# Projection steps, rotation engine and first loads in a four-layer trunk: one change in four places

## The chip, the cores and the metric

The kernel runs on one core of one Trainium2 chip. The metric is the device time of one execution in microseconds. A run's time is a little longer than the span of its trace, which reaches from the first to the last instruction.

## The reference

The reference is a trunk of four residual layers over 512 tokens with 1024 features, all in float32, each with an RMS norm ahead of it.

- An even mixer: stick-breaking attention with 16 heads of width 64, strictly causal. Its weights are `sigmoid(z)` times the product of `sigmoid(-z)` over the later keys in front of the query.
- A SwiGLU feed-forward layer with 2816 hidden features: `(silu(h Wg) * (h Wu)) Wd`.
- An odd mixer: differential attention with 8 heads. Every head has two query-key maps of width 64 and one v of width 128. q and k get an RMS norm per group of 64, then a partial rotation of their first 16 features by the positions; the two softmax maps are combined as `a1 - lam * a2`; the head's output is normed again.
- A second SwiGLU layer.

## The kernel before, in words

**Precision.** Every float32 product is made of three TensorE products of rounded halves (`mm3`, line 215): high times high, high times low, low times high. So each operand exists as a pair `hi`, `lo`. Weights are split on arrival in one of two ways. `wload` (line 105) fetches the raw weights over SP's queue into a tile of tag "raw" (two buffers), rounds them on ScalarE to `hi`, and subtracts on VectorE to get `lo`. `wload_acc` (line 115) writes `hi` and `-hi` on ScalarE and then lets GpSimd's queue fetch the weights a second time with an accumulating transfer, which leaves `lo`. Five pairs of 1024 columns are there at a time (`WB`).

**The order of the work.** The kernel is written as one program for a scheduler which makes the semaphores and the order on each engine. The place in the program is the priority: an engine takes the earliest instruction that is ready by the scheduler's own timeline, so later work can run ahead of its place where engines would be idle. Each engine then runs that order as it is. Tiles of one tag share a fixed number of buffers. Later work is also mixed in by hand: `fillers` holds generators of matmul steps, `fill(n)` (line 227) takes n steps from them, `flush` (line 235) takes all up to one generator.

**The start** (lines 86 to 95 and 390 to 478). x comes as 8 tiles of 128 x 512 over SP's queue, mixed with the first pair's q and k weights in quarters (lines 402 to 408). ScalarE and VectorE make the 16 halves of the scaled x (`Norm.scaled`), which stay in tiles of tag "t" of the pool with `HP` = 26 buffers. TensorE runs the first q and k. Then come the first v chunk (`v_chunk(0)`, lines 428 to 449, weights by `wload_acc` on line 446) and the norm's root and broadcast (`Norm.finish`, line 183).

**A head of attention** is a call of `attend` (line 371): scores and weights of the four query blocks from the last to the first (`weigh(3)` to `weigh(0)`), between them the end of the head before (`after`), the transposes of the weights (`wt_bank`), four calls `fill(steps[i])`, and `middle`. The weights times v (`av`) follow.

**The odd layer** (`diff_layer`, line 707) works on four pairs of heads. `qk_steps(c)` (line 750) makes q and k of pair c: 4 token blocks of 512 columns with two yields each, so 8 steps; each block is evicted (line 756), squared into a tile of tag "tmp" (line 758, three buffers in the whole kernel) and reduced (line 759). After the last step come the root, the scaling of the whole tile (line 769) and the rotation: for q and for k four VectorE instructions, two on 128 columns and two on 256 (lines 786 to 789). `v_steps(c)` (line 729) has 4 steps. `head_stacks` (line 792) transposes one head's q and k and splits them into stacks; the k stack is completed by two copies on GpSimd's queue (line 334). `weights` (line 802) takes the softmax maps; its results lie in tiles `e1` with 4 buffers. `head_out` (line 847) finishes a head: transposes, squares into a tile of tag "tmp" (line 861), norm, transposes and halves.

The loop over heads (lines 907 to 926) sets the places. `counts[hd]` says how many steps stand at each of the four calls of `fill`: in the even head 2, 1, 2, 1 and in the odd head 2, 1, 1, 1 for the first three pairs; in the last two heads 1 each, which take the first half of the output projection. `after` of a head is `head_out` of the head before. In an odd head `middle` first flushes the next pair's `qk_steps` and then makes the next head's stacks. `before` flushes the pair's own v.

Of the kernel before, what the change touches and what calls it, by code (L numbers as in the profile page):

```python
# [12 lines left out]
F32 = mybir.dt.float32  # L13
# [4 lines left out]
ALU = mybir.AluOpType  # L18
# [3 lines left out]
P = 128  # L22
S = 512
# [8 lines left out]
ROT = 16  # L32
RSQRT_MAGIC = float(0x5F3759DF)
TCK = dict(schedule_with_timeline_sim=True)
HP = 26
WB = 5
THIRDS = ((0, 8), (8, 8), (16, 6))
TWO_PI_A = 6.28125
# [5 lines left out]
def trunk(  # L44
# [26 lines left out]
    nc = tc.nc  # L71
    V, A, G, T = nc.vector, nc.scalar, nc.gpsimd, nc.tensor
# [10 lines left out]
    x = [xp.tile([P, S], F32, name=f"x{i}") for i in range(KT)]  # L83
# [31 lines left out]
    def wload_acc(ap):  # L115
        raw = raw_tile()
        hi, lo = pair()
        nc.sync.dma_start(out=raw, in_=ap)
        A.activation(hi, raw, AF.Copy)
        A.activation(lo, hi.bitcast(F32), AF.Copy, scale=-1.0)  # L120
        G.dma_start(out=lo, in_=ap, accum_op=ALU.add)
        return hi, lo
# [267 lines left out]
    def stick_layer(norm, nxt):  # L390
        h = norm.h
        with ExitStack() as st:
            vp = st.enter_context(tc.tile_pool(name="vp0", bufs=2))
            sp = st.enter_context(tc.tile_pool(name="sp0", bufs=2))
            at = st.enter_context(tc.tile_pool(name="at0", bufs=2))
# [6 lines left out]
            for j in range(4):  # L402
                c = slice(j * 256, (j + 1) * 256)
                for i, (raw, (hi, lo)) in enumerate(zip(raws, first)):
                    nc.sync.dma_start(out=raw[:, c], in_=wqk0[8 * i][:, c])
                for i in (2 * j + 1, 2 * j + 2):
                    if i < KT:
                        nc.sync.dma_start(out=x[i], in_=xT[i])
            nc.sync.dma_start(out=gf, in_=g_ffn)
            for j in range(4):  # L410
                c = slice(j * 256, (j + 1) * 256)
# [16 lines left out]
            def v_chunk(c):  # L428
                v = vp.tile([P, TT, 4, P], F32R, tag="v", name="v0")

                def evac(t, ps):
                    rs = norm.rstd[:, t : t + 1]
                    src = ps.rearrange("p (h d) -> p h d", d=64)
                    A.activation(v[:, t, :, 0:64], src, AF.Copy, scale=rs)
                    V.scalar_tensor_tensor(
                        v[:, t, :, 64:128],
                        src,
                        rs,
                        v.bitcast(F32)[:, t, :, 0:64],
                        op0=ALU.mult,  # L440
                        op1=ALU.subtract,
                    )

                def steps():
                    yield from nat_steps(
                        [wload_acc(wv0[c, j]) for j in range(2)], h, evac, 256, 1
                    )

                return v, steps()
# [257 lines left out]
    def diff_layer(norm, nxt):  # L707
        h = norm.h
        with ExitStack() as st:
# [40 lines left out]
            def qk_steps(c, out):  # L750
                t_ = qp.tile([P, TT, S], F32, tag="qk", name="qk_nat")
                ss = sm.tile([P, 32], F32, tag="rs_v", name="qk_ss")

                def evac(t, ps):
                    norm_ready()
                    A.activation(t_[:, t], ps, AF.Copy, scale=norm.rstd[:, t : t + 1])
                    sq = tmp.tile([P, S], F32, tag="tmp", name="qk_sq")
                    A.activation(sq, t_[:, t], AF.Square)
                    V.reduce_sum(
                        ss[:, t * 8 : (t + 1) * 8],  # L760
                        sq.rearrange("p (g d) -> p g d", d=64),
                        axis=AX.X,
                    )

                yield from nat_steps([wload_kept(("wqk", c, j)) for j in range(4)], h, evac, 512, 2)
                V.tensor_scalar(ss, ss, 1.0 / 64, EPS, op0=ALU.mult, op1=ALU.add)
                u = rsqrt(ss, 32)
                f3 = t_.rearrange("p t (g d) -> p (t g) d", d=64)
                V.tensor_tensor(
                    f3, f3, u.unsqueeze(2).to_broadcast([P, 32, 64]), op=ALU.mult  # L770
                )
                for which in range(2):
                    f4 = t_[:, :, which * 256 : which * 256 + 256].rearrange(
                        "p t (g d) -> p t g d", d=64
                    )
                    ta, tb = (
                        r.unsqueeze(2).to_broadcast([P, TT, 4, ROT]) for r in rot[which]
                    )
                    mt = tmp.tile([P, S], F32, tag="tmp", name="rope")
                    m = [  # L780
                        mt[:, i * 256 : i * 256 + 256].rearrange(
                            "p (t g d) -> p t g d", t=TT, d=ROT
                        )
                        for i in range(2)
                    ]
                    V.tensor_tensor(m[1][:, :, :, 0:8], f4[:, :, :, 8:16], tb[:, :, :, 0:8], op=ALU.mult)
                    V.tensor_tensor(m[1][:, :, :, 8:16], f4[:, :, :, 0:8], tb[:, :, :, 8:16], op=ALU.mult)
                    V.tensor_tensor(m[0], f4[:, :, :, 0:ROT], ta, op=ALU.mult)
                    V.tensor_tensor(f4[:, :, :, 0:ROT], m[0], m[1], op=ALU.add)
                out.append(t_)  # L790

            def head_stacks(qk, hh):
# [9 lines left out]
            def weights(q2, k2, ss, qt):  # L802
                n = (qt + 1) * P
                nm = sm.tile([P, 2], F32, tag="nm", name="nm")
                e1 = at.tile([P, S], F32, tag="e1", bufs=4, name="e1")
                e2 = at.tile([P, S], F32, tag="e2", name="e2")
                for e, o in ((0, e1), (1, e2)):
                    ps = scp.tile([P, S], F32, tag="sc", name="sc")
                    scores(ps, q2, k2, e, qt)
                    V.memset(ps[0:64, n - 64 : n], NEG)  # L810
                    V.reduce_max(nm[:, e : e + 1], ps[:, :n], axis=AX.X, negate=True)
                    A.activation(
                        o[:, :n],
                        ps[:, :n],
                        AF.Exp,
                        bias=nm[:, e : e + 1],
                        accum_out=ss[:, e, qt : qt + 1],
                    )
                c = sm.tile([P, 2], F32, tag="c", name="c")
                V.reciprocal(c[:, 0:1], ss[:, 1, qt : qt + 1])  # L820
                V.tensor_scalar(
                    c[:, 1:2], ss[:, 0, qt : qt + 1], nlam, c[:, 0:1], op0=ALU.mult, op1=ALU.mult
                )
                V.scalar_tensor_tensor(
                    e1[:, :n], e2[:, :n], c[:, 1:2], e1[:, :n], op0=ALU.mult, op1=ALU.add
                )
                return e1
# [76 lines left out]
                gens["v", c] = v_steps(c, vs)  # L904
                fillers.extend((gens["qk", c], gens["v", c]))
            last = out_first(1, og)
            counts = ((2, 1, 2, 1), (2, 1, 1, 1)) * 3 + ((1, 1, 1, 1), (1, 1, 1, 1))
            for hd in range(8):
                hh = hd % 2
                c = hd // 2  # L910
# [109 lines left out]
```

## Time and profile before

| what | value |
|---|---|
| median of 3 runs | 1301.82 us (1300.54 to 1305.36) |
| profiled execution, its own time | 1301.36 us |
| its span | 1299.6 us |
| TensorE busy (PE) | 1239.7 us, 95% |
| VectorE busy (DVE) | 740.2 us, 57% |
| ScalarE busy (ACT) | 568.2 us, 44% |
| GpSimd busy (POOL) | 80.8 us, 6% |
| mean granted clock of TensorE | 0.979 |

The profile names engines as PE (matmuls), PEld (weight loads of TensorE), DVE, ACT, POOL and SP. Instructions are given by the line of the kernel, the tile they write and the tiles they read; a line can be that of a helper. A clock of 1.00 is TensorE's full 2.4 GHz, 0.50 is 1.2 GHz. Matmuls are pipelined, so the duration of one is longer than the distance to the next. By the trace the even mixer fills the first 270 us or so, the first feed-forward layer reaches to about 635 us, the odd mixer to about 931 us, and the second feed-forward layer to the end.

### The profile page before, as it was taken

The numbers are of one execution on the slowest core, as the hardware profiler recorded it, in microseconds if no ns is written. First come the engines' busy times: TensorE is split into PE (matmuls) and PEld (weight loads), VectorE is DVE, ScalarE is ACT, GpSimd is POOL, SyncE is SP. The second block draws the span as 40 slices with busy tenths as digits, with TensorE's granted clock in tenths as the row PEclk, the third lists the DMA queues.
The fourth block names the chain that finished last, engine by engine and source line by source line (L and its number), as shares of the span: only waits on it lengthen the run. The fifth ranks groups of instructions, "written<-read, shape, count | busy, mean of one in ns | idle before, by whom it ended". The sixth has DMA issues, their size and how long they took to land.

```text
span 1299.6 us, 16000 instructions
## 1 busy us (share of the span) xinstructions
PE 1239.7 (95%) x5974; PEld 1032.3 (79%) x5974; DVE 740.2 (57%) x1426; ACT 568.2 (44%) x964; POOL 80.8 (6%) x132
## 2 busy tenths in 40 slices
PE   6999999889999999999999997968899999999998
PEld 5888888778888888888888887745688888888886
DVE  5567868597544554455535657677754434443442
ACT  7777887455332432334324445345443223321220
POOL 1211111000000000000000000000000000000000
PEclk8999999999999999999999998979899999999999
DMA  7965768238776777766557352501222323332222
GB/s 222 220 148 134 169 143 191 58 97 275 247 227 244 242 246 231 243 233 227 196 194 227 131 158 90 174 17 33 97 100 97 95 97 98 98 97 97 93 73 77
DMA packets 61133, 199.44 MB, mean 153 GB/s; under 512 B 8320, under 2 KB 9344, under 8 KB 61056
## 3 DMA queue, kind: packets, MB, share of 16 engines
q1 hardware_dynamic: 42768, 140.74, 33.0%
q0 software_dynamic: 18144, 57.68, 16.8%
q8 instruction: 47, 0.77, 0.2%
q14 instruction: 30, 0.25, 0.1%
q10 hardware_dynamic: 144, 0.01, 0.0%
HBM read 154.36 MB, written 35.65 MB: 146 GB/s over the span
## 4 chain that ended last, share of the span: by engine, by line
PE 90%; DVE 3%; ACT 3%; DMA 2%; issue 1%; SPq 0%; POOL 0%; DVEq 0%; ACTq 0%; POOLq 0%
PE ps_d L217 6%; PE ps_d L216 6%; PE ps_d L218 6%; PE ps_g L218 6%; PE ps_g L216 6%; PE ps_g L217 6%; PE ps_u L218 6%; PE ps_u L216 6%; PE ps_u L217 6%; PE ps_nat L216 4%; PE ps_nat L217 4%; PE ps_nat L218 4%; PE ps_o L216 2%; PE ps_o L217 2%; PE ps_o L218 2%; PE tp L358 2%
## 5 line engine op out<-in xcount | busy, mean ns | idle before, releaser
L109 ACT ACTIVATE whi<-wraw 128x1024 fp32r<-128x1024 f32 (+1 forms) x136 | 138.6, 1033 | 355.8 <-PE ps_d L217 82.4
L110 DVE TENSOR_TENSOR wlo<-wraw,whi 128x1024 fp32r<-128x1024 f32 (+1 forms) x136 | 161.9, 1192 | 106.1 <-ACT whi L109 50.5
L217 PE MATMUL ps_d<-alo,whi 128*128 128x512 f32 x352 | 139.1, 396 | 0.0
L218 PE MATMUL ps_d<-ahi,wlo 128*128 128x512 f32 x352 | 139.0, 396 | 0.0
L216 PE MATMUL ps_d<-ahi,whi 128*128 128x512 f32 x352 | 138.9, 396 | 0.0
L216 PE MATMUL ps_u<-hhi,whi 128*128 128x512 f32 x352 | 137.7, 391 | 0.3 <-DVE x L298 0.2
L218 PE MATMUL ps_g<-hhi,wlo 128*128 128x512 f32 x352 | 137.6, 391 | 0.0
L217 PE MATMUL ps_g<-hlo,whi 128*128 128x512 f32 x352 | 137.2, 390 | 0.0
L218 PE MATMUL ps_u<-hhi,wlo 128*128 128x512 f32 x352 | 137.1, 390 | 0.0
L217 PE MATMUL ps_u<-hlo,whi 128*128 128x512 f32 x352 | 137.1, 390 | 0.0
L216 PE MATMUL ps_g<-hhi,whi 128*128 128x512 f32 x352 | 136.7, 390 | 0.0
L217 PE MATMUL ps_nat<-wlo,hhi 128*128 128x256 f32 (+1 forms) x384 | 124.7, 325 | 7.0 <-DMA wlo<-in_wv 7.0
L216 PE MATMUL ps_nat<-whi,hhi 128*128 128x256 f32 (+1 forms) x384 | 124.5, 326 | 1.1 <-DVE k L453 1.0
L218 PE MATMUL ps_nat<-whi,hlo 128*128 128x256 f32 (+1 forms) x384 | 124.7, 325 | 0.0
L606 DVE TENSOR_TENSOR x<-x,ps_d 128x512 f32<-128x512 f32 x48 | 32.8, 687 | 97.2 <-PE ps_d L218 97.1
L217 PEld LDWEIGHTS ps_nat<-wlo,hhi 128*128 128x128 f32 x384 | 74.1, 193 | 12.5 <-DMA wlo<-in_wv 7.2
L216 PEld LDWEIGHTS ps_nat<-whi,hhi 128*128 128x128 f32 x384 | 74.0, 193 | 7.0 <-DVE k L453 1.2
L217 PEld LDWEIGHTS ps_d<-alo,whi 128*128 128x128 f32 x352 | 66.2, 188 | 15.9
L218 PEld LDWEIGHTS ps_d<-ahi,wlo 128*128 128x128 f32 x352 | 66.2, 188 | 15.9
L216 PEld LDWEIGHTS ps_d<-ahi,whi 128*128 128x128 f32 x352 | 66.2, 188 | 15.9
L218 PEld LDWEIGHTS ps_nat<-whi,hlo 128*128 128x128 f32 x384 | 74.1, 193 | 5.1 <-issue 0.2
L216 PEld LDWEIGHTS ps_u<-hhi,whi 128*128 128x128 f32 x352 | 66.1, 188 | 14.9 <-ACT whi L109 0.6
(206 smaller groups left out, 2328.5 us busy)
## 6 DMA issues: line engine op xcount, KB each, us to landing
wraw<-in_wgu SPq DMA_DIRECT2D x88, 512.0 KB, 3.6
wraw<-in_wd SPq DMA_DIRECT2D x32, 512.0 KB, 3.6
k<-k POOLq DMA_DIRECT2D x32, 256.0 KB, 3.3
praw<-in_wqk SPq DMA_DIRECT2D x16, 512.0 KB, 5.7
kept_wqk<-whi POOLq DMA_DIRECT2D x16, 512.0 KB, 5.5
kept_wqk<-wlo POOLq DMA_DIRECT2D x16, 512.0 KB, 6.6
whi<-kept_wqk SPq DMA_DIRECT2D x16, 512.0 KB, 6.3
wlo<-kept_wqk SPq DMA_DIRECT2D x16, 512.0 KB, 5.9
```

The lines of the kernel that those rows point to most:

```text
L109: A.activation(hi[:, :cols], raw[:, :cols], AF.Copy)
L110: V.tensor_tensor(lo[:, :cols], raw[:, :cols], hi.bitcast(F32)[:, :cols], op=ALU.subtract)
L216: T.matmul(ps, lh[0], rh[0], start=first, stop=False)
L217: T.matmul(ps, lh[0], rh[1], start=False, stop=False)
L218: T.matmul(ps, lh[1], rh[0], start=False, stop=last)
L358: T.transpose(tp[:, o : o + P], w[qt][:, kt * P : (kt + 1) * P], ident)
L606: V.tensor_tensor(x[m], x[m], ps, op=ALU.add)
```

## The change

Five edits are made.

- `counts` for the first three pairs of the odd layer become 3, 3, 3, 3 in the even head and 0, 0, 0, 0 in the odd head.
- The eight rotation instructions of a pair move from VectorE to GpSimd.
- x[1] to x[7] are fetched over GpSimd's queue instead of SP's.
- The two weight tiles of the even layer's first v chunk are split by `wload` instead of `wload_acc`; the other three chunks stay.
- `e1` gets a fifth buffer, and `HP` goes from 26 to 25 (one buffer of either kind is 2 KB a partition).

```diff
--- before.py
+++ after.py
@@ -32,7 +32,7 @@
 ROT = 16
 RSQRT_MAGIC = float(0x5F3759DF)
 TCK = dict(schedule_with_timeline_sim=True)
-HP = 26
+HP = 25
 WB = 5
 THIRDS = ((0, 8), (8, 8), (16, 6))
 TWO_PI_A = 6.28125
@@ -405,7 +405,7 @@
                     nc.sync.dma_start(out=raw[:, c], in_=wqk0[8 * i][:, c])
                 for i in (2 * j + 1, 2 * j + 2):
                     if i < KT:
-                        nc.sync.dma_start(out=x[i], in_=xT[i])
+                        G.dma_start(out=x[i], in_=xT[i])
             nc.sync.dma_start(out=gf, in_=g_ffn)
             for j in range(4):
                 c = slice(j * 256, (j + 1) * 256)
@@ -443,7 +443,11 @@
 
                 def steps():
                     yield from nat_steps(
-                        [wload_acc(wv0[c, j]) for j in range(2)], h, evac, 256, 1
+                        [(wload_acc if c else wload)(wv0[c, j]) for j in range(2)],
+                        h,
+                        evac,
+                        256,
+                        1,
                     )
 
                 return v, steps()
@@ -783,10 +787,10 @@
                         )
                         for i in range(2)
                     ]
-                    V.tensor_tensor(m[1][:, :, :, 0:8], f4[:, :, :, 8:16], tb[:, :, :, 0:8], op=ALU.mult)
-                    V.tensor_tensor(m[1][:, :, :, 8:16], f4[:, :, :, 0:8], tb[:, :, :, 8:16], op=ALU.mult)
-                    V.tensor_tensor(m[0], f4[:, :, :, 0:ROT], ta, op=ALU.mult)
-                    V.tensor_tensor(f4[:, :, :, 0:ROT], m[0], m[1], op=ALU.add)
+                    G.tensor_tensor(m[1][:, :, :, 0:8], f4[:, :, :, 8:16], tb[:, :, :, 0:8], op=ALU.mult)
+                    G.tensor_tensor(m[1][:, :, :, 8:16], f4[:, :, :, 0:8], tb[:, :, :, 8:16], op=ALU.mult)
+                    G.tensor_tensor(m[0], f4[:, :, :, 0:ROT], ta, op=ALU.mult)
+                    G.tensor_tensor(f4[:, :, :, 0:ROT], m[0], m[1], op=ALU.add)
                 out.append(t_)
 
             def head_stacks(qk, hh):
@@ -802,7 +806,7 @@
             def weights(q2, k2, ss, qt):
                 n = (qt + 1) * P
                 nm = sm.tile([P, 2], F32, tag="nm", name="nm")
-                e1 = at.tile([P, S], F32, tag="e1", bufs=4, name="e1")
+                e1 = at.tile([P, S], F32, tag="e1", bufs=5, name="e1")
                 e2 = at.tile([P, S], F32, tag="e2", name="e2")
                 for e, o in ((0, e1), (1, e2)):
                     ps = scp.tile([P, S], F32, tag="sc", name="sc")
@@ -904,7 +908,7 @@
                 gens["v", c] = v_steps(c, vs)
                 fillers.extend((gens["qk", c], gens["v", c]))
             last = out_first(1, og)
-            counts = ((2, 1, 2, 1), (2, 1, 1, 1)) * 3 + ((1, 1, 1, 1), (1, 1, 1, 1))
+            counts = ((3, 3, 3, 3), (0, 0, 0, 0)) * 3 + ((1, 1, 1, 1), (1, 1, 1, 1))
             for hd in range(8):
                 hh = hd % 2
                 c = hd // 2
```

## Rows read from the trace of the kernel before

**Rows 1.** Stretches: length, busy us of PE, PEld, DVE, ACT, POOL; granted clock; DMA; GB/s.

```profile
25.00:30.00 5.00, 2.21 (x10) 2.21 (x11) 0.00 (x0) 2.11 (x2) 0.86 (x1) 0.50 1.04 258
...
690.00:742.00 52.00, 52.00 (x324) 46.64 (x323) 33.97 (x109) 24.11 (x64) 1.17 (x2) 1.00 0.55 190
742.00:906.00 164.00, 135.97 (x711) 110.58 (x710) 116.92 (x376) 77.23 (x219) 6.95 (x12) 0.91 0.32 98
```

**Rows 2.** Order of time at the start: start us, us, engine, line, operation [idle before].

```profile
17.59 1.06 ACT L119 ACTIVATE whi<-wraw 128x1024 fp32r<-128x1024 f32 x1 [1.80 <-DMA wraw<-in_wv]
...
20.07 1.07 POOL L121 DMA_DIRECT2D wlo<-in_wv  x1 [18.76 <-ACT wlo L120]
...
20.18 0.40 PE L218 MATMUL ps_k<-hhi,wlo 128*128 128x512 f32 x1
...
27.79 0.58 PE L217 MATMUL ps_nat<-wlo,hhi 128*128 128x256 f32 x1 [6.98 <-DMA wlo<-in_wv]
...
33.08 1.31 PE L211 MATMUL ps_bc<-dg,ones 128*128 128x512 f32 x2
```

**Rows 3.** TensorE in time: first av product of heads 0, 1, 2, 3, 7.

```profile
718.64 0.39 PE L216 MATMUL av<-wt_hi,v1h 128*128 128x512 f32 x1
...
739.90 0.40 PE L216 MATMUL av<-wt_hi,v1h 128*128 128x512 f32 x1
...
785.96 0.39 PE L216 MATMUL av<-wt_hi,v1h 128*128 128x512 f32 x1
...
799.25 0.77 PE L216 MATMUL av<-wt_hi,v1h 128*128 128x512 f32 x1
...
903.26 0.48 PE L216 MATMUL av<-wt_hi,v1h 128*128 128x512 f32 x1
```

**Rows 4.** ScalarE in time: pair 1's eviction and square, pair 3's square.

```profile
694.42 0.69 ACT L756 ACTIVATE qk_nat<-ps_nat,rstd 128x512 f32<-128x512 f32 x1
...
727.67 0.37 ACT L861 ACTIVATE o_sq<-tn,rs 128x128 f32<-128x128 f32 x1
...
728.01 0.64 ACT L758 ACTIVATE qk_sq<-qk_nat 128x512 f32<-128x512 f32 x1
...
849.54 1.16 ACT L758 ACTIVATE qk_sq<-qk_nat 128x512 f32<-128x512 f32 x2
```

**Rows 5.** Waits of ScalarE, 690 to 906 us: total us, times, longest us.

```profile
ACT e L812 <- PE tp L358: 2.3, 3, 1.1
```

**Rows 6.** Order of time in the even layer around the fifth pair's output.

```profile
187.05 0.69 DVE L533 TENSOR_TENSOR olo<-o,ohi 128x512 fp32r<-128x512 f32 x1
...
190.67 0.39 PE L216 MATMUL ps_k<-hhi,whi 128*128 128x512 f32 x1
...
225.51 0.67 DVE L516 TENSOR_TENSOR o<-av,avt 64x512 f32<-64x512 f32 x1
```

**Rows 7.** Two source lines of the rotation: duration ns min/median/max.

```profile
L786 DVE TENSOR_TENSOR rope<-qk_nat,rot x8: 280/284/291, 666.1 to 861.2; 128x128 f32<-128x128 f32 x8
...
L789 DVE TENSOR_TENSOR qk_nat<-rope x8: 415/418/423, 667.9 to 862.3; 128x256 f32<-128x256 f32 x8
```

**Rows 8.** Order of time around pair 0's rotation and first stack.

```profile
663.45 2.29 DVE L769 TENSOR_TENSOR qk_nat<-qk_nat,rs_u 128x2048 f32<-128x2048 f32 x1
...
667.92 0.75 DVE L789 TENSOR_TENSOR qk_nat<-rope 128x256 f32<-128x256 f32 x2
...
672.61 0.60 PE L798 MATMUL tqk<-ident,qk_nat 128*128 128x128 f32 x4
```

**Rows 9.** Costliest groups on the page: the low halves of the weights.

```profile
L110 DVE TENSOR_TENSOR wlo<-wraw,whi 128x1024 fp32r<-128x1024 f32 (+1 forms) x136 | 161.9, 1192 | 106.1 <-ACT whi L109 50.5
```

**Rows 10.** DMA issue to landing: x to 20 us, wlo 14 to 45.

```profile
DMA to landing us min/median/max: 2.8/4.3/4.6
...
DMA to landing us min/median/max: 6.8/8.3/9.5
```

**Rows 11.** Pair 0's projection and v: the stretch for ps_nat alone.

```profile
634.74:669.56 34.82, 34.07 (x193) 29.55 (x193) 1.44 (x3) 4.16 (x7) 1.00 0.45 161
```

## The prediction

> **What bounds the kernel now.** I read the page's busy shares first (TensorE is busy for 95% of the span, so a change has to remove TensorE idle time or time at the lower clock), then the stretches, to find where that idle time lies. Two places are left. One is the start: in 25 to 30 us TensorE runs at a granted clock of 0.50, which is the 1.2 GHz level, and is busy for less than half of the stretch. The other is the odd layer from its second head on: in 742 to 906 us TensorE is busy for 136.0 of 164 us at a mean clock of 0.91, while from 690 to 742 it had no gap at all [rows 1]. Then I read the order of time in both places.
>
> At the start TensorE ends the first projections at 20.58 us and stands 6.98 us at the second term of v's product, because wlo of v's first weights is fetched by an accumulating transfer. GpSimd issues that at 20.07 us, though the raw weights had been there at 17.59 us, when ScalarE began to round them. The products then run at the lower clock up to the broadcast of the norm at 33.08 us [rows 2].
>
> In the odd layer the cadence of the heads tells more than any single wait. The av products of heads 0 and 1 begin 21.3 us apart (718.64 and 739.90). Head 2 comes 46.1 us after head 1, and head 3 13.3 us after head 2; that long-short pattern stands three times. From head 1 to head 7 the mean is (903.26 - 739.90)/6 = 27.2 us [rows 3]. The reason is in ScalarE's order: the last block of pair 1's q and k was evicted at 694.42 us, but its square was taken only at 728.01 us, directly behind the squares of head 0's output (727.67). The same stands twice more, for pairs 2 and 3, the last at 849.54 us [rows 4]. The tiles of tag "tmp" are given out in the order of the program, and in the program the last projection steps of a pair stand in the odd head behind the call that finishes the head before. So norm, rotation and stacks of the next pair cannot begin before that head is finished, and there is nothing left then to put on TensorE.
>
> **The change, part by part.** The sum goes against the profiled execution, 1301.36 us (span 1299.6 and 1.8 around it); it lies 0.46 us under the median of 1301.82.
>
> Projection steps. A pair's projection has 8 steps and its v 4. With counts of 3 in the even head and 0 in the odd one all 12 stand in the even head, so the four squares of a pair come ahead of that head's own finish and behind the odd head's before it. Pair 1's rotation can end some 30 us sooner (728.01 against 694.42), and pairs 2 and 3 each get one head, 21 us or more, of slack where they have none now. The long interval goes. What is late next is TensorE itself: its 136.0 us of work in these six heads are 22.7 us a head [rows 1, 3]. VectorE's 116.9 us, less two rotations, are 18.5 us a head. I take 23 us a head: (27.2 - 23) x 6 = 25 us. From below: 0, if another wait fills the long interval. From above: at full clock TensorE's 136.0 us shrink by about 9%, to 20.6 us a head, near the 21.3 already shown; 6 x 6.6 = 40 us. I lie on TensorE's present busy time and not on the 20.6, because some idle time stays. What follows the last head I leave as it is. In the odd heads no projection steps are left in program order; they are covered by the next pair's steps, which TensorE already runs ahead of their place (no gap in 690 to 742). If that cover is gone, it is the second rival.
>
> The fifth e1 buffer. ScalarE's exponential waits for the transposes of the head before three times, 2.3 us together [rows 5]. That is the most it shows; it is inside the 23 us. It is paid by a 26th residual buffer: the low half of pair 4's output in the even layer must now wait for the first h tile. It is written at 187.05 us and would come some 4 us later, when pair 7's key projection has begun (190.67); the next pair but one writes into the buffer that it reads only at 225.51 us [rows 6]. So it costs nothing; if that slack were gone, some 4 us.
>
> Rotation on GpSimd. Four instructions like L786 (0.284 us) and four like L789 (0.418) are 2.8 us a pair on VectorE [rows 7], and leave it. On GpSimd no row shows such an operation. Bounds for the pair: 2.8 us, as on VectorE, and 8 x 2.29 = 18.3, if each took as long as VectorE's longest operation on this path, L769 with 2048 columns [rows 8]; on columns of 128 and 256 I lie near the lower end, 6 us. Only pair 0 has it on the way: its last rotation ends at 668.67 us, the stacks' transposes begin at 672.61 [rows 8], and 3.9 us of slack hide 6 - 2.8. Behind it on GpSimd stand the two copies of each k stack; those of the odd head are issued ahead of it, those of the next even head need it anyway. I put it at 0; up to 15.4 - 3.9 = 11.5 us. The Trainium skill (GPSIMD Engine Reference, section 3.1, Elementwise, side-by-side cycle accounting) speaks against this part: an addition of two float32 tensors of 2048 columns takes 4497 ns there against 2293 on VectorE, about twice. VectorE's figure agrees with L769's 2.29 us here [rows 8]; GpSimd's no row here shows. By that rule a pair would take about 5.6 us, an estimate, and the sum would stay as it is.
>
> v's first weights. Without the two transfers the low half is ready at 17.59 + 1.06 + 1.19 (L110's mean [rows 9]) = 19.84 us, before TensorE is free at 20.58. The 6.98 us go. So does the lower clock that followed the gap: the products from 27.79 to 33.08 us, 5.3 us, would take half, 2.6 us less. Against it stand 2.4 us of VectorE work ahead of the norm's root, and what is late next: the weights of the next projection, whose own accumulating transfers land 6.8 to 9.5 us after issue [rows 10] and are wanted some 9 us sooner. They gain from the 1 MB that no longer moves beside them. I take 8.5 us; bounds 4 and 9.6. The even layer behind it keeps TensorE busy, so the shift lasts.
>
> x over GpSimd's queue. Seven issues leave SP. On GpSimd the first issue took 1.07 us, and the engine had been idle for 18.76 us before it [rows 2], so all seven can go out ahead of everything else there. x lands 2.8 to 4.6 us after issue now, the slowest accumulating transfer of GpSimd's queue took 9.5 [rows 10]: between 1.8 us sooner and 4.9 us later for the first x. I take 0, near x's own rows, since both queues move the same bytes at the same time. The first weights come sooner on SP, which is worth nothing while ScalarE rounds both x and them in turn.
>
> Sum: 25 + 8.5 = 33.5 us, so 1268.
>
> **The rivals.**
> Only the start pays. Another thing in program order, such as v's two buffers or the two PSUM banks of the projections, fills the long interval between odd and even head. For it: the scheduler makes its own order, and no row shows the new one. Against it: the square's wait, 33.6 us for pair 1, stands three times in the same place [rows 4]. Time: 1301.4 - 8.5 = 1293.
>
> The projection goes ahead of the even head's own scores, and the odd head stands uncovered. If the plan keeps program order, the 12 steps (34.1 us of products for pair 0 [rows 11]) come between the score blocks of the even head: 34.1 + 13.3, its own work at the shortest interval shown, and then 13.3 for the odd head, which has nothing beside it. That is 60.7 us a pair against 2 x 27.2 now, 6.3 us more for each of the three pairs with a projection behind them: 1301.4 + 18.9 - 8.5 = 1312. It decides from the point where TensorE no longer runs a pair ahead. Against it: in 690 to 742 us TensorE has no gap though the program gives these heads fewer steps than that [rows 1], so order is only a preference.
>
> GpSimd's rotation is exposed. At the upper bound of 18.3 us pair 0's stacks start 11.5 us late, and nothing later gives it back: 1280. The Trainium skill (the same page, section 8, Key points) adds that GpSimd shares its SBUF interfaces with VectorE where VectorE reads two SBUF inputs; no run here shows what that costs.
>
> The start does not pay. x lands late from the software queue, or the first projection's weights do, and 8.5 us become 0 while the heads gain: 1276.
>
> **How the numbers follow.** Chances: forecast 0.64 (by itself 1252 to 1284: 9.6 + 40 us at the one end, 4 + 13 us, half of the cadence's gain, at the other); only the start 0.17, of which 0.07 within 0.5%; own scores behind the projection 0.07, slower; rotation exposed 0.07; no start 0.05. A measurement of this kernel can tell about 0.5%, 6.5 us, from no change. Faster 0.64 + 0.10 + 0.07 + 0.05 = 0.86, same 0.07, slower 0.07. The range takes in the upper bounds and the start alone, 1252 to 1294; the slower rival stays outside.
>
> **What would show it.** Right: no wait of TensorE for wlo at v's first product, and a clock of 1.00 in 25 to 35 us; the square of the last block of a pair behind the finish of the odd head before, not of its own even head; av products of heads 1 to 7 about 23 us apart without the long-short pattern; TensorE busy over 90% from the second head to the last. Wrong: long intervals that remain, with another releaser ahead of the stacks' transposes; TensorE idle in odd heads with VectorE busy; transposes of the stacks that wait for GpSimd; a first projection after v that waits for its own transfer.

## The result and the profile after

The changed kernel takes 1266.1 us (median of 4 runs, 1263.76 to 1268.86) against 1301.55 before: a ratio of 0.9723, interval 0.9695 to 0.9751. The forecast was 1268 in a range of 1252 to 1294. Its profiled execution is the slowest of the four, 1268.86 us, with a span of 1267.0, so the same 1.8 us lie around the span as before. The total is right, and that is partly luck: one of the two large terms under it was put too small and the other did not come at all, and the errors cancel.

Busy shares on the page of the changed kernel:

```profile
PE 1225.4 (97%) x5974; PEld 1024.5 (81%) x5974; DVE 732.2 (58%) x1396; ACT 566.8 (45%) x962; POOL 101.4 (8%) x169
```

TensorE has the same work and less of it at the lower clock (1225.4 us busy against 1239.7); GpSimd has 20 us more. The stretches of the changed kernel show where (columns: stretch, length, busy us of PE, PEld, DVE, ACT, POOL with instructions, granted clock, DMA share, GB/s):

```profile
25.00:30.00 5.00, 4.84 (x36) 4.01 (x35) 3.04 (x8) 4.90 (x7) 1.29 (x2) 1.00 0.77 188
30.00:35.00 5.00, 5.00 (x44) 5.00 (x43) 3.03 (x5) 3.68 (x7) 2.60 (x4) 1.00 1.01 256
40.00:45.00 5.00, 1.05 (x5) 0.55 (x3) 0.00 (x0) 2.01 (x3) 0.88 (x1) 0.94 1.20 242
45.00:50.00 5.00, 4.58 (x12) 3.88 (x13) 2.13 (x3) 4.97 (x8) 0.00 (x0) 0.50 1.04 274
742.00:873.00 131.00, 122.20 (x712) 105.00 (x711) 105.54 (x351) 71.77 (x209) 14.90 (x26) 0.97 0.40 123
```

Against [rows 1], the hole at 25 to 30 us is closed and the clock there is 1.00. The same kind of hole, with the 0.50 clock behind it, now stands at 40 to 50 us. In the odd layer, 742 to 873 us reaches from head 1 to just behind the av of head 7, as 742 to 906 did before: 33 us shorter, TensorE busy for 93% at 0.97 instead of 83% at 0.91.

**The odd layer.** TensorE in time, first av product of heads 0, 1, 2, 3 and 7:

```profile
723.25 0.48 PE L216 MATMUL av<-wt_hi,v1h 128*128 128x512 f32 x1
...
743.68 0.40 PE L216 MATMUL av<-wt_hi,v1h 128*128 128x512 f32 x1
...
772.75 0.39 PE L216 MATMUL av<-wt_hi,v1h 128*128 128x512 f32 x1
...
791.73 0.40 PE L216 MATMUL av<-wt_hi,v1h 128*128 128x512 f32 x1
...
870.73 0.50 PE L216 MATMUL av<-wt_hi,v1h 128*128 128x512 f32 x1 [0.69 <-ACT wt_hi L361]
```

From head 1 to head 7 the mean is (870.73 - 743.68)/6 = 21.2 us, 27.2 before [rows 3]. A weaker long-short pattern is left (29.1, then 19.0). From its first projection product to the start of the last output product the layer took 635.72 to 898.20, 262.5 us; before it was 634.74 to 930.68, 295.9. That is 33.5 us less: 36.3 in the six intervals, against which heads 0 and 1 come 2.8 us later after the layer's start, for which twelve steps now stand in head 0 (that these are the reason is not shown).

ScalarE and VectorE in time, pair 1's last block and the scaling of its tile:

```profile
695.39 0.69 ACT L760 ACTIVATE qk_nat<-ps_nat,rstd 128x512 f32<-128x512 f32 x1
696.11 0.64 ACT L762 ACTIVATE qk_sq<-qk_nat 128x512 f32<-128x512 f32 x1
...
703.31 2.29 DVE L773 TENSOR_TENSOR qk_nat<-qk_nat,rs_u 128x2048 f32<-128x2048 f32 x1
```

Pair 1's square follows its eviction at once; before, it came 33.6 us behind it [rows 4]. For pairs 2 and 3 a wait is left. ScalarE in time, pair 2's last eviction, the last square of head 1's output, pair 2's squares:

```profile
738.79 0.69 ACT L760 ACTIVATE qk_nat<-ps_nat,rstd 128x512 f32<-128x512 f32 x1 [3.03 <-PE ps_nat L218]
...
751.05 0.21 ACT L865 ACTIVATION_READ_ACCUMULATOR o_sq<-tn,rs 128x1 f32 x1
751.14 1.16 ACT L762 ACTIVATE qk_sq<-qk_nat 128x512 f32<-128x512 f32 x2
```

The squares come directly behind the finish of the odd head before, as the forecast's sign had it. For pair 3 it is the same (800.12 behind 800.03).

**The start.** TensorE in time: the first product, v's first low-half product, the end of the second pair's q, the first scores; then, of the tile `k`, the copies that complete pair 0's k stack:

```profile
6.39 0.79 PE L216 MATMUL ps_q<-hhi,whi 128*128 128x512 f32 x1 [6.39 <-ACT whi L414]
...
21.48 0.37 PE L217 MATMUL ps_nat<-wlo,hhi 128*128 128x256 f32 x1
...
40.66 0.39 PE L218 MATMUL ps_q<-hhi,wlo 128*128 128x512 f32 x1
45.42 0.77 PE L340 MATMUL sc<-k,q 128*128 128x512 f32 x1 [4.36 <-DMA k<-k]
```

```profile
L334 POOL DMA_DIRECT2D k<-k x2: 606/614/623, 33.6 to 34.3; - x2
...
DMA to landing us min/median/max: 11.7/11.8/11.9
```

The same first scores, and the landing of the same two copies, in the kernel before:

```profile
45.07 0.39 PE L340 MATMUL sc<-k,q 128*128 128x512 f32 x1
```

```profile
DMA to landing us min/median/max: 6.0/6.0/6.0
```

The wait for wlo (6.98 us [rows 2]) is gone, and 4.36 us in front of the scores stand in its place, so the first scores begin no sooner. TensorE had done everything else by 41.05 us; the copies, issued at 33.59 us, landed only 11.7 to 11.9 us later. Before, the same two were issued at 37.86 us and landed after 6.0. GpSimd in time, first in the changed kernel, then in the one before, shows what went out just ahead of them:

```profile
26.45 0.91 POOL L121 DMA_DIRECT2D wlo<-in_wqk  x1 [20.86 <-DVE rstd L201]
29.62 0.88 POOL L121 DMA_DIRECT2D wlo<-in_wqk  x1 [2.26 <-ACT wlo L120]
32.36 0.87 POOL L121 DMA_DIRECT2D wlo<-in_wv  x1 [1.86 <-PE ps_nat L218]
33.59 1.33 POOL L334 DMA_DIRECT2D k<-k  x2 [0.37 <-DVE k L312]
```

```profile
30.00 0.86 POOL L121 DMA_DIRECT2D wlo<-in_wqk  x1 [3.97 <-ACT wlo L120]
36.27 0.86 POOL L121 DMA_DIRECT2D wlo<-in_wv  x1 [5.40 <-ACT wlo L120]
37.86 1.32 POOL L334 DMA_DIRECT2D k<-k  x2 [0.73 <-DVE k L312]
```

Three accumulating transfers of 512 KB were issued in the 8 us ahead of the copies; before, two were (30.00 and 36.27 us). Besides, the first product starts at 6.39 instead of 5.16 us. It waits for the first rounded weights, and ScalarE shows why they are late (changed kernel, then before):

```profile
5.41 0.63 ACT L173 ACTIVATE sq<-x 128x512 f32<-128x512 f32 x1 [0.60 <-DMA x<-in_xT]
5.94 0.40 ACT L414 ACTIVATE whi<-wraw 128x256 fp32r<-128x256 f32 x1
```

```profile
4.70 0.71 ACT L414 ACTIVATE whi<-wraw 128x256 fp32r<-128x256 f32 x2
```

The first quarter of the raw weights was there at 3.89 us, as before (3.92). But ScalarE's order now has the square of x[1] ahead of it, and that waits for x[1], which landed at 5.39 us, no later than before (5.62).

The odd layer starts at 635.72 against 634.74: of the 8.5 us forecast for the start, nothing has arrived. One execution could mislead here, since two kernels below with the same start (the rotation on VectorE, and four e1 buffers) wait 2.6 us for the copies and begin the scores at 43.58 and 43.46 us. But nothing of this lasts: in the five profiled executions with the changed start the odd layer begins at 631.7 to 635.7 us, in the four with the old one at 632.8 to 635.4, 634.0 in the mean of either.

**The rotation.** Two source lines of it on GpSimd (duration ns min/median/max), the end of pair 0's rotation, and where its stack then begins:

```profile
L790 POOL TENSOR_TENSOR rope<-qk_nat,rot x8: 447/450/462, 666.9 to 816.7; 128x128 f32<-128x128 f32 x8
```

```profile
L793 POOL TENSOR_TENSOR qk_nat<-rope x8: 726/732/753, 669.9 to 818.9; 128x256 f32<-128x256 f32 x8
```

```profile
669.93 1.43 POOL L793 TENSOR_TENSOR qk_nat<-rope 128x256 f32<-128x256 f32 x2
```

```profile
674.49 0.60 PE L802 MATMUL tqk<-ident,qk_nat 128*128 128x128 f32 x4
```

Four instructions like the first and four like the second are 4 x 0.450 + 4 x 0.732 = 4.7 us a pair, where 6 was put; from its first start to its last end pair 0's rotation took 4.5 us (666.86 to 671.36). Pair 0's first transpose comes 10.1 us behind the scaling of the tile (664.42), 9.2 before [rows 8]. But the rotation had ended 3.1 us sooner (671.36), and TensorE was busy with other products up to the transpose, so nothing of it is exposed. By the Trainium skill (GPSIMD Engine Reference, section 3.1, Elementwise) a float32 addition of 2048 columns takes about twice VectorE's time; here a multiplication on 128 columns takes 450/284 = 1.6 times as long as on VectorE and the addition on 256 columns 732/418 = 1.75 times [rows 7].

### The profile page after: what moved, and what is told of

Same layout as the page of the kernel before. It is cut to its first block, busy times and chain, and to the rows that moved or that the text cites. A ratio compares the mean times of both kernels' runs of the same rounds, so it can differ in the third digit from the quotient of the medians.

```text
span 1267.0 us, 16005 instructions
## 1 busy us (share of the span) xinstructions
PE 1225.4 (97%) x5974; PEld 1024.5 (81%) x5974; DVE 732.2 (58%) x1396; ACT 566.8 (45%) x962; POOL 101.4 (8%) x169
## 4 chain that ended last, share of the span: by engine, by line
PE 89%; DVE 3%; issue 3%; DMA 3%; ACT 1%; POOL 0%; SPq 0%; DVEq 0%; POOLq 0%; ACTq 0%
PE ps_d L216 6%; PE ps_d L217 6%; PE ps_d L218 6%; PE ps_u L216 6%; PE ps_g L216 6%; PE ps_u L218 6%; PE ps_g L217 6%; PE ps_u L217 6%; PE ps_g L218 6%; PE ps_nat L216 4%; PE ps_nat L217 4%; PE ps_nat L218 4%; PE ps_o L216 2%; PE ps_o L217 2%; PE ps_o L218 2%
## 5 line engine op out<-in xcount | busy, mean ns | idle before, releaser
L216 PEld LDWEIGHTS ps_g<-hhi,whi 128*128 128x128 f32 x352 | 66.4, 189 | 14.1 <-issue 0.2
L217 PEld LDWEIGHTS ps_g<-hlo,whi 128*128 128x128 f32 x352 | 66.2, 188 | 14.0 <-issue 0.2
```

Of the source, the lines that this page charges most:

```text
L216: T.matmul(ps, lh[0], rh[0], start=first, stop=False)
L217: T.matmul(ps, lh[0], rh[1], start=False, stop=False)
```

## The experiments

Twelve kernels ran, in three groups, each beside the kernel before (medians 1301.61, 1300.54 and 1301.4 us).

**1. Which part pays.** Only the new counts:

```diff
-            counts = ((2, 1, 2, 1), (2, 1, 1, 1)) * 3 + ((1, 1, 1, 1), (1, 1, 1, 1))
+            counts = ((3, 3, 3, 3), (0, 0, 0, 0)) * 3 + ((1, 1, 1, 1), (1, 1, 1, 1))
```

> The kernel before with the new counts alone. Theory (the last squares of a pair waited for a tile of tag tmp that the program gives out behind the finish of the even head): the odd layer, 296.2 us from its first projection product (634.7) to the end of its last output product (930.9), falls by 20 to 33 us, so 1269 to 1282 us in all; the start is as before. Rival (the counts pay only together with the rotation on GpSimd and the fifth e1 buffer): the odd layer falls by at most 12 us, 1290 us or more.

Measured: 1270.7 us (0.9767, interval 0.9746 to 0.9787). The heads come (871.29 - 743.91)/6 = 21.2 us apart.

The change with the old counts (all but the edit above):

> The changed kernel with the old counts. Theory: the long intervals between odd and even heads stay, the odd layer takes 288 to 296 us, 1293 to 1302 us in all. Rival (the rotation on GpSimd and the fifth e1 buffer carry much of the gain): 1285 us or less.

Measured: 1306.07 us (1.0033, interval 1.0019 to 1.0047), 4.5 us more than before, with this at TensorE in the first 60 us (total us, times, longest):

```profile
PE sc L340 <- DMA k<-k: 3.4, 1, 3.4
```

Only the split of v's first weights:

```diff
-                        [wload_acc(wv0[c, j]) for j in range(2)], h, evac, 256, 1
+                        [(wload_acc if c else wload)(wv0[c, j]) for j in range(2)], h, evac, 256, 1
```

> The kernel before with v's first weights split on VectorE, and nothing else. Theory (the 7 us are won at v and lost again at pair 0's k copies, which wait in the queues behind weights): TensorE waits 2 to 6 us for the k copies ahead of the first scores, which begin at 44 to 46 us as before, and the time is within 3 us of before, 1298 to 1304 us. Rival (the start was lost to x over GpSimd's queue): 1291 to 1295 us.

Measured: 1302.7 us (1.0007, interval 0.9995 to 1.0019). v's low-half product starts at 20.97 us without a wait, and 2.6 us of wait for `k<-k` stand ahead of the scores. What follows: the step counts alone carry most of the gain, 30.9 us of 35.5. The start's edit removes its wait and is worth nothing, even with x on SP's queue.

**2. Why the projection's tail waited.** The forecast blamed the tag "tmp". The kernel before, with the squares and the rotation in a tag of their own:

```diff
-HP = 26
+HP = 25
-                    sq = tmp.tile([P, S], F32, tag="tmp", name="qk_sq")
+                    sq = tmp.tile([P, S], F32, tag="qsq", bufs=1, name="qk_sq")
-                    mt = tmp.tile([P, S], F32, tag="tmp", name="rope")
+                    mt = tmp.tile([P, S], F32, tag="qsq", bufs=1, name="rope")
```

> The kernel before with its old counts; the squares of the projection and the rotation get a tag of their own with one buffer (and HP is 25 to make room). Theory (the tile was what they waited for): the last square of pair 1 comes within 10 us of its eviction though its place in the program is behind head 0's finish; the odd layer falls by 15 to 30 us, 1271 to 1287 us. Rival (the place of the steps in the program, as the priority, was what held them): the square stays some 30 us late and the time stays within 5 us of before, 1296 us or more.

Measured: 1304.11 us (1.0016, interval 1.0005 to 1.0027): no gain. The order of time on ScalarE, then on VectorE, says why:

```profile
692.27 0.69 ACT L756 ACTIVATE qk_nat<-ps_nat,rstd 128x512 f32<-128x512 f32 x1 [0.88 <-PE ps_nat L218]
693.00 0.63 ACT L758 ACTIVATE qk_sq<-qk_nat 128x512 f32<-128x512 f32 x1
```

```profile
694.89 0.17 DVE L766 TENSOR_SCALAR qk_ss<-qk_ss 128x32 f32<-128x32 f32 x1
...
727.50 0.14 DVE L142 TENSOR_SCALAR rs_u<-o_ss 128x4 int32<-128x4 int32 x1
727.54 0.17 DVE L142 TENSOR_SCALAR rs_u<-qk_ss 128x32 int32<-128x32 int32 x1
...
731.12 2.29 DVE L769 TENSOR_TENSOR qk_nat<-qk_nat,rs_u 128x2048 f32<-128x2048 f32 x1
```

The square is now free. The chain stops one step further on: the sums are ready at 695.06, but the root's first instruction comes at 727.54, directly behind the root of head 0's output norm. Its tiles `rs_u` and `rs_t` are of tags that both norms share. So all shared tags of the chain were given tags of their own, with the old counts kept:

```diff
-    def rsqrt(v, n):
-        u = sm.tile([P, 32], F32, tag="rs_u", name="rs_u")[:, :n]
-        t = sm.tile([P, 32], F32, tag="rs_t", name="rs_t")[:, :n]
+    def rsqrt(v, n, own=""):
+        u = sm.tile([P, 32], F32, tag="rs_u" + own, bufs=1 if own else 4, name="rs_u")[:, :n]
+        t = sm.tile([P, 32], F32, tag="rs_t" + own, bufs=1 if own else 4, name="rs_t")[:, :n]
...
-                ss = sm.tile([P, 32], F32, tag="rs_v", name="qk_ss")
+                ss = sm.tile([P, 32], F32, tag="rs_v_qk", bufs=1, name="qk_ss")
...
-                u = rsqrt(ss, 32)
+                u = rsqrt(ss, 32, "_qk")
```

(HP is 24 here; the squares and the rotation as in the kernel above.)

> As e2_own_tag, and the root of the projection's norm gets tiles of its own too (rs_u, rs_t and rs_v were shared with head_out's root; HP is 24 to make room). Old counts. Theory (every shared tag is given out in the order of the program; in e2 the next such tile held the chain): pair 1's scaling of the whole tile, at 731 to 734 us so far, comes before 710 us, the long intervals go, 1270 to 1287 us. Rival (the place of the steps is a priority on the engines, whatever the tiles): the scaling stays near 730 us and the time at 1296 us or more.

Measured: 1269.23 us (0.9748, interval 0.9713 to 0.9783). VectorE in time, pair 1:

```profile
698.17 0.16 DVE L142 TENSOR_SCALAR rs_u<-qk_ss 128x32 int32<-128x32 int32 x1
...
703.29 2.29 DVE L769 TENSOR_TENSOR qk_nat<-qk_nat,rs_u 128x2048 f32<-128x2048 f32 x1
```

With the old counts the scaling comes at 703.29 us, as with the new ones (703.31). The steps' places in the program are the old ones here, so it was the tiles and not the places as such that held the chain. This settles the mechanism: the tiles of a shared tag are handed out in program order, and one such tag anywhere in the chain holds all of it. (Which of the three small tags had to be freed was not taken apart.) For pairs 2 and 3 the squares now follow their evictions too (738.70 behind 737.75 for pair 2), and yet the time is no better than with the new counts, so the waits that those leave are no large term. Moving the steps ahead in the program and taking the chain out of the shared tags are two cures for one wait.

Both cures together, on the changed kernel (the tags as above, e1 with 4 buffers, HP 24):

> The changed kernel with tags of their own for the squares, the rotation and the three small tiles of the norm, and four e1 buffers. Theory (with the projection steps in the even head the chain of the norm is already free, and TensorE is the bound): 1262 to 1268 us, at most 3 us better. Rival (tags and steps each take away a part of the waits): 1255 to 1260 us.

Measured: 1267.6 us (0.974, interval 0.9726 to 0.9753), within the theory's range; beside the kernel with four e1 buffers and the new counts (1271.09, below) it is 3.5 us. There is little left to take from this wait.

**3. The two parts costed at nothing.** The changed kernel with the rotation back on VectorE (the four `G.tensor_tensor` as `V.tensor_tensor`):

> The changed kernel with the rotation back on VectorE. Theory (the rotation lies off the path in either place): within 3 us of the changed kernel, 1263 to 1269 us. Rival A (GpSimd's slower rotation, 4.7 us a pair against 2.8, lies on the way to the stacks): 2 to 8 us faster, 1258 to 1263. Rival B (VectorE's relief of 11 us pays): 1270 to 1277 us.

Measured: 1271.82 us (0.9772, interval 0.9742 to 0.9802).

The changed kernel with four e1 buffers:

```diff
-HP = 25
+HP = 26
-                e1 = at.tile([P, S], F32, tag="e1", bufs=5, name="e1")
+                e1 = at.tile([P, S], F32, tag="e1", bufs=4, name="e1")
```

> The changed kernel with four e1 buffers in place of five. Theory (the fifth buffer is worth at most the 2.3 us of waits that the forecast gave it): 1264 to 1269 us, the av products of the odd layer's heads still about 21 us apart. Rival (the buffer lets each head's scores start earlier, 0.5 to 1 us a head): 1270 to 1275 us, the heads 22 us apart or more.

Measured: 1271.09 us (0.9767, interval 0.9751 to 0.9782): the rival's band, but not its cadence, (871.34 - 743.94)/6 = 21.2 us.

| rotation | e1 buffers | us |
|---|---|---|
| VectorE | 4 (counts alone) | 1270.7 |
| GpSimd | 4 | 1271.09 |
| VectorE | 5 | 1271.82 |
| GpSimd | 5 (the change, and two variants of its start below) | 1266.1, 1265.24, 1265.33 |

Neither edit alone shows a gain; with both, the time is about 5 us lower. (The intervals of the two sides touch or overlap a little; that three kernels stand on either side carries this reading. The counts alone also lack the start's edits.) The difference lies in the odd layer: it took 265.4, 264.6 and 268.9 us in the profiled executions of the first three rows, and 257.4 to 262.5 in the five kernels with both edits (the changed one and the four of the next group). ScalarE's waits over 690 to 900 us, for the counts alone, the rotation on VectorE, four buffers, and the changed kernel:

```profile
ACT e L812 <- DVE nm L811: 19.9, 23, 2.6
```

```profile
ACT e L816 <- DVE nm L815: 24.8, 23, 5.3
```

```profile
ACT e L816 <- DVE nm L815: 22.8, 21, 2.4
...
ACT e L816 <- PE tp L358: 10.1, 3, 5.2
```

```profile
ACT e L816 <- DVE nm L815: 17.4, 22, 2.3
```

With the rotation on VectorE the exponential waits longer for a maximum from VectorE, and with four buffers it waits also for a free buffer: 10.1 us in three waits, where the kernel before showed 2.3 [rows 5] and the changed one shows none. But this does not explain the 5 us. The counts alone, which lack both edits and are as slow, wait 19.9 us for maxima and never for a buffer. And each of the three slower kernels has another order of instructions on TensorE in the odd layer than the changed one, so an order that came out better by chance is a rival that no run tests. Why both edits together are faster is open.

**4. Why the start did not pay.** The changed kernel, in which pair 0's two k copies go over ScalarE's queue instead of GpSimd's (`nc.scalar.dma_start` on line 334, for pair 0 alone):

> The changed kernel with pair 0's two k copies over ScalarE's queue instead of GpSimd's. Theory (the copies wait in GpSimd's queue behind accumulating transfers issued before them): they land within 6 us of issue instead of 11.8, the wait of 4.4 us ahead of the first scores falls below 1 us, the lower clock behind it goes too; 1259 to 1263 us. Rival (the 16 DMA engines are full there, whichever queue): landing stays at 9 us or more, the wait at 3 us or more, 1264 to 1269 us.

Measured: 1265.24 us (0.9721, interval 0.9693 to 0.975). The copies still land 8.8 to 11.0 us after issue, so GpSimd's queue is at most a small part of it; the wait is 1.8 us, which neither the theory nor the rival had.

The changed kernel with x on SP's queue again:

> The changed kernel with x back on SP's queue. Theory (x over GpSimd's queue moved the first product from 5.2 to 6.4 us and the rest of the start by the same): first product at 5.0 to 5.3 us, v's first product 1 us sooner, but the k copies still decide the first scores, so within 2 us of the changed kernel, 1264 to 1268 us. Rival (x in GpSimd's queue delays what follows in that queue, the k copies among it): 3 to 6 us faster, 1260 to 1263 us.

Measured: 1265.33 us (0.9722, interval 0.9692 to 0.9753). The first product starts at 5.17 us again, and 2.6 us of wait for the copies remain, as long as in the two kernels of the third group with x on GpSimd's queue.

The changed kernel with fewer bytes at that time, since the second pair's weights no longer arrive twice:

```diff
-                yield from gemm_steps(ps, wload_acc(wqk0[p]), h)
+                yield from gemm_steps(ps, (wload_acc if p > 1 else wload)(wqk0[p]), h)
...
-                yield from gemm_steps(ps, wload_acc(wqk0[8 + p]), h)
+                yield from gemm_steps(ps, (wload_acc if p > 1 else wload)(wqk0[8 + p]), h)
```

> The changed kernel, in which the weights of the first layer's second pair of heads are also loaded by the plain weight load in place of the load that accumulates. Theory (the k copies of pair 0 are late because the DMA engines are full between 30 and 50 us): with fewer bytes in that stretch the copies land within 8 us, TensorE waits under 1 us for them, and the time is 1260 to 1264 us. Rival (what the start gains is given back later in the first layer): the wait goes, but the time stays at 1264 to 1268 us.

Measured: 1262.95 us (0.9715, interval 0.9702 to 0.9729). The tile `k` in 30 to 41 us, and a wait and two stretches of TensorE:

```profile
L334 POOL DMA_DIRECT2D k<-k x2: 590/606/622, 35.6 to 36.4; - x2
...
DMA to landing us min/median/max: 4.9/5.6/6.3
```

```profile
PE ps_bc L211 <- DVE dg L204: 2.2, 1, 2.2
```

```profile
40.00:45.00 5.00, 5.00 (x25) 4.23 (x24) 0.71 (x1) 3.88 (x6) 0.94 (x2) 1.00 1.11 250
45.00:50.00 5.00, 5.00 (x26) 4.12 (x25) 4.59 (x8) 4.82 (x10) 0.85 (x1) 1.00 1.00 282
```

Only one accumulating transfer (33.06 us) is issued in the 8 us ahead of the copies. They land in 5.6 us instead of 11.8, the wait ahead of the first scores is gone and the clock stays at 1.00. VectorE, which now splits more weights, is late next: 2.2 us for the diagonal of the norm's broadcast.

The same with x on SP's queue:

> The kernel with the second pair's plain weight loads, and x again over SP's queue as before the change. Theory (both halves of the start's loss, the late x and the full DMA engines, are repaired): first product near 5.2 us, no wait over 1 us for k, 1258 to 1263 us. Rival (given back later in the first layer): 1264 to 1268 us.

Measured: 1260.93 us (0.9692, interval 0.9678 to 0.9705; 1260.72 to 1261.92). First product at 5.11 us, no wait for k in the first 60 us, 3.3 us for the diagonal. It is the fastest kernel of the study, some 5 us under the changed one.

What follows: the late copies come from the transfers of weights issued ahead of them. All fourteen profiled executions bear this out: with three accumulating transfers issued in the 8 us ahead the copies took 8.8 to 11.9 us (eight kernels, the one over ScalarE's queue included), with two 6.0 to 8.2 (four), with one 4.8 to 6.3 (the last two). Whether the kind of transfer matters or only the bytes is not separated: counting plain ones too, 4 or 5, 3 or 4, and 1 of these 512 KB transfers were under way when the first copy was issued.

What the repair is worth in time is less clear. The interval of the first of the two kernels lies within that of the changed one. With x on SP's queue it is 1260.93 against 1265.33 us, which is clearer: the executions do not overlap (1260.72 to 1261.92 against 1263.34 to 1266.96). TensorE's idle time and its loss at the lower clock (over stretches of 5 us, the busy time times what the clock lacks to 1.00) fall in the first 60 us from 13.0 + 3.1 us in the kernel before to 9.8 + 0 in the first of the two. But the odd layer begins at 631.39 and 632.29 us, 3.4 and 2.5 us sooner than before, which hardly leaves the spread of 631.7 to 635.7 given above. The rest of their lead over the changed kernel lies in the odd layer, 259.6 and 259.0 us against 262.5, though its code is the same in all three; with x on SP's queue alone it was 257.4. In the first of the two TensorE's order there is that of the changed kernel, so its 2.9 us are a difference between executions (the changed kernel's profile is the slowest of its four, this one the fastest of its five); with x on SP's queue the order is another. What the order is worth is open.

## Why the prediction was right, and where not

- **The cause in the odd layer: right in kind, too narrow in place.** "The tiles of tag "tmp" are given out in the order of the program" holds, but freeing that tag alone gave nothing (1304.11), and freeing rs_u, rs_t and rs_v as well gave 1269.23. The rule is not one of this tag alone. The forecast stopped at the first wait that it could read; the second was hidden behind it.
- **The size of this term: too small.** "I take 23 us a head", 25 us in all; the six intervals gave 21.2 us each and the layer 33.5 us. The step that failed is "I lie on TensorE's present busy time and not on the 20.6". The busy time of before held work at the lower clock, which went with the idle time (0.91 to 0.97 over the six heads). It lies within the bound of 40 us. The counts alone give 1301.61 - 1270.7 = 30.9 us.
- **Rotation and fifth buffer: perhaps not nothing.** Both were put at 0, as the absence of harm. With both the time is about 5 us lower than with either alone; whether the edits themselves or the order of instructions that came with them did this is open. With the old counts the edits, start included, cost 4.5 us (1306.07). The rotation on GpSimd took 4.7 us a pair where 6 was put, and none of it is exposed. (Its upper bound is 18.3 - 2.8 - 3.9 = 11.6 us, not 11.5.)
- **v's first weights: the cover was misnamed.** The 6.98 us went and the clock was 1.00 from 20 to 40 us, as forecast. "They gain from the 1 MB that no longer moves beside them" failed: what is late next is not the next projection's weights but pair 0's k copies. They were issued 4.3 us sooner and took 5.8 us longer, because the next weights' transfers had moved up to just ahead of them. 8.5 us became none. The rival "the start does not pay" had a chance of 0.05 and named the right kind of cause, a late transfer, but the one that decided is neither of the two that it named.
- **x over GpSimd's queue: 0 was put, 1.2 us came out,** within the bounds of -1.8 and +4.9. (In all seven profiles with x on this queue the first product starts at 6.4 to 7.2 us, in the seven others at 5.1 to 5.3.) The cause is ScalarE's new order and not a late x[1]: that ScalarE "rounds both x and them in turn" was right, but the turn changed. With x on SP's queue again the first product regains it; the whole time, 1265.33, cannot be told from the changed kernel's.
- **The other rivals fell.** Only the start pays (1293): the opposite happened. The projection ahead of the own scores (1312): visible at most as the 2.8 us by which heads 0 and 1 come later. Rotation exposed (1280): not seen.

So 33.4 us were forecast from the profiled execution and 35.5 came between the medians: 25 became 31 from the steps, some 5 came with rotation and buffer for a reason that stays open, and 8.5 became 0. That the sum came within 2 us of the forecast is luck; that the odd layer carries the gain, and by which wait, is not. The range says little by itself: it also held the rival in which only the start pays.

## What to carry to other kernels

Where a chain waits for something that seems unrelated to its data, list every tile tag that it shares with the work in front of it in program order, not only the first that shows in the trace; give the chain its own tags or move it ahead. An edit that removes a wait for a transfer pulls the next transfer forward into the same busy stretch, so cost that one by what will be issued just ahead of it. Where every edit makes the scheduler draw up another order, a few us of difference do not yet price the edit: put several kernels on either side, and see whether every slow one shows the wait that is meant to explain them.

## What the hardware showed

- Landing time of one and the same 256 KB copy from SBUF to SBUF: 4.8 to 6.3, 6.0 to 8.2 and 8.8 to 11.9 us, with one, two and three accumulating transfers issued in the 8 us ahead. The DMA share does not tell them apart: in the kernel with the second pair's plain loads, in the one before and in the changed one it is 1.0 or more while they move (1.06 before in 40 to 45 us). The Trainium skill (DMA: Bandwidth & Descriptors, section Anatomy of one DMA) fits a GpSimd transfer with 2.0 us plus its bytes at 436 GB/s, an estimate of 2.6 us for this copy; in these three kernels it took 2.2 to 4.5 times that in the median (5.6, 6.0 and 11.8 us).
- The seven tiles of x that were moved landed 7.0 us after issue in the median over GpSimd's queue, 4.4 over SP's, but they were issued closer together (within 3.7 us instead of 6.3), and the last was there at 13.1 and 12.7 us. An issue kept GpSimd for 0.54 us.
- After the 4.36 us in which TensorE stood, the next stretch ran at a granted clock of 0.50; with x on SP's queue 2.6 us of standing at the same place were followed by 1.00, and with the rotation on VectorE or four e1 buffers the same 2.6 us by 0.76 and 0.84. In the fastest kernel 3.3 us of standing, ahead of the diagonal, were followed by 0.66 over 30 to 35 us.
